# Softmax over rows of 512: three loads of 32 rows per partition, and the multiplications of six groups moved to GpSimd

## Chip, cores, metric

One core of a Trainium2 chip. The metric is the device time of one execution in microseconds (us).

## The reference

A softmax over the last axis, x of 16 x 1024 x 512 in fp32, result in fp32:

```python
x_max = np.max(x, axis=-1, keepdims=True)
exp_x = np.exp(x - x_max)
return (exp_x / np.sum(exp_x, axis=-1, keepdims=True)).astype(np.float32)
```

16,384 rows of 2 KB: 33.55 MB are read and 33.55 MB written. Each of the 128 partitions holds 128 rows.

## The kernel before

SBUF holds 96 rows per partition in one tile, so the last 32 rows are loaded over the first ones once these are stored. `CHUNKS` lists the loads as (rows, place). Work goes in groups of up to 8 rows: maxima on VectorE, exponentials with sums on ScalarE, reciprocal and multiplication on VectorE, then a store. The loads go out on the queue of SyncE, the stores on ScalarE's.

```python
CHUNKS = [
    (3, 0), (5, 3), (8, 8), (16, 16), (16, 32), (16, 48), (16, 64), (16, 80), (16, 0), (16, 16),
]
EARLY = 8                       # loads issued at the start
AFTER_STORE = {2: [8], 3: [9]}  # load 8 follows the store of chunk 2, load 9 that of chunk 3
STORE_ROWS = {3: 8, 4: 8, 5: 8} # stores of 8 rows in these chunks, else the whole chunk
# ... cut ...
    def scale(g):
        k, a, b, since = groups[g]
        recip = stats.tile([P, b - a], F32, name="recip", tag="recip")
        nc.vector.reciprocal(out=recip, in_=sums[g])
        for r in range(a, b):
            nc.vector.tensor_scalar_mul(
                out=place[k][:, r, :],
                in0=place[k][:, r, :],
                scalar1=recip[:, r - a : r - a + 1],
            )
        if since is not None:
            nc.scalar.dma_start(out=dst[k][:, since:b, :], in_=place[k][:, since:b, :])
        # ... cut: the loads of AFTER_STORE ...
        for g, (k, a, _, _) in enumerate(groups):
            # ... cut: groups 1 to 3 finish the group before first ...
            rowmax(g)
            exps(g)
            if waiting is not None:
                scale(waiting)
            waiting = g
```

The rows of one partition lie together in HBM, so a load of 16 rows is one run of 32 KB per partition, and the trace shows it as one packet of that size per partition, spread over 16 DMA engines.

## Time and profile before

| | before |
|---|---|
| median time | 161.45 us (six runs, 161.40 to 161.84) |
| span of the profiled execution | 159.6 us |
| bytes moved | 67.13 MB, 421 GB/s over the span |
| VectorE busy | 123.9 us, 78% |
| ScalarE busy | 93.3 us, 58% |
| GpSimd busy | 0.2 us |

The two slice rows, the chain and the groups are shown in the prediction below. In the lines of the profile DVE is VectorE, ACT ScalarE, POOL GpSimd and DMA a transfer; SPq is the queue of SyncE, which issues the loads.

### The profile page before, as it was taken

Reading aid. Unit: us, or ns where it says so; the run is one execution under the profiler, and the core shown is the slowest. Engines: PE = TensorE matmul, PEld = TensorE weight load, DVE = VectorE, ACT = ScalarE, POOL = GpSimd, SP = SyncE. Lnnn points to the kernel's source line nnn. Section 1 sums busy time; section 2 is a strip of 40 time slices with the busy share of each in tenths; the row PEclk is TensorE's granted clock in tenths of the full one; section 3 lists DMA queues with packets and bytes.
Section 4 is the critical chain, followed back from the end, with each engine's and each line's share of the span. In section 5 each row is a group of like instructions: output and inputs, shape, how many; then the busy total and the mean of one; then the engine's idle time right before and its main releaser. Section 6 shows DMA issues by size and latency. Waiting matters only on the chain.

```text
span 159.6 us, 511 instructions
## 1 busy us (share of the span) xinstructions
DVE 123.9 (78%) x162; ACT 93.3 (58%) x257; POOL 0.2 (0%) x4
## 2 busy tenths in 40 slices
DVE  0482880799699999999999999999999999853000
ACT  0717119207994959595958687776868595940000
POOL 0000000000000000000000000000000000000000
DMA  7999999899999999999899999999999999999993
GB/s 267 443 456 432 399 414 466 375 404 467 411 446 411 485 419 396 439 411 493 378 448 439 411 497 411 405 444 402 435 444 485 411 402 468 435 402 419 485 411 164
DMA packets 3315, 67.13 MB, mean 421 GB/s; under 512 B 368, under 2 KB 368, under 8 KB 624
## 3 DMA queue, kind: packets, MB, share of 16 engines
q1 hardware_dynamic: 1440, 33.56, 49.4%
q10 hardware_dynamic: 1872, 33.56, 49.0%
q14 instruction: 3, 0.02, 0.0%
HBM read 33.55 MB, written 33.55 MB: 421 GB/s over the span
## 4 chain that ended last, share of the span: by engine, by line
DVE 71%; ACT 14%; issue 3%; DMA 3%; DVEq 0%; ACTq 0%
DVE shift L125 39%; DVE held L147 30%; ACT held L133 14%; DMA held<-in_x_dram 3%; DVE recip L145 2%; DVEq L199 0%; ACTq L133 0%
## 5 line engine op out<-in xcount | busy, mean ns | idle before, releaser
L133 ACT ACTIVATE held<-held,shift 128x512 f32<-128x512 f32 x128 | 90.5, 708 | 43.4 <-DVE shift L125 33.3
L125 DVE TENSOR_REDUCE shift<-held 128x8 f32<-128x4096 f32 (+2 forms) x17 | 70.7, 4164 | 4.6 <-DMA held<-in_x_dram 4.6
L147 DVE TENSOR_SCALAR held<-held,recip 128x512 f32<-128x512 f32 x128 | 52.2, 482 | 0.6
L133 ACT ACTIVATION_READ_ACCUMULATOR held<-held,shift 128x1 f32 x128 | 23.9, 187 | 0.0
L145 DVE RECIPROCAL recip<-sums 128x8 f32<-128x8 f32 (+2 forms) x17 | 3.3, 195 | 15.8 <-ACT held L133 15.8
L133 ACT ACT_TABLE_LOAD x1 | 1.3, 1283 | 4.7 <-DMA held<-in_x_dram 4.7
L188 POOL MEMSET const-bfloat16-1.0<- 128x1 bf16 x1 | 0.1, 103 | 0.0
L188 POOL MEMSET const-uint8-127<- 128x1 uint8 x1 | 0.1, 102 | 0.0
L188 POOL MEMSET const-float32-1.0<- 128x1 f32 x1 | 0.1, 100 | 0.0
L188 POOL MEMSET const-float32-0.0<- 128x1 f32 x1 | 0.1, 99 | 0.2 <-issue 0.2
## 6 DMA issues: line engine op xcount, KB each, us to landing
held<-in_x_dram SPq DMA_DIRECT2D x7, 4096.0 KB, 41.8
out_dram<-held ACTq DMA_DIRECT2D x4, 4096.0 KB, 20.9
out_dram<-held ACTq DMA_DIRECT2D x7, 2048.0 KB, 35.3
held<-in_x_dram SPq DMA_DIRECT2D x1, 2048.0 KB, 11.7
held<-in_x_dram SPq DMA_DIRECT2D x1, 1280.0 KB, 7.2
out_dram<-held ACTq DMA_DIRECT2D x1, 1280.0 KB, 19.9
held<-in_x_dram SPq DMA_DIRECT2D x1, 768.0 KB, 4.6
out_dram<-held ACTq DMA_DIRECT2D x1, 768.0 KB, 15.6
```

The source lines that it names most:

```text
L125: nc.vector.reduce_max(out=shift[g], in_=place[k][:, a:b, :], axis=AX, negate=True)
L133: nc.scalar.activation(out=place[k][:, r, :], in_=place[k][:, r, :], func=EXP, bias=shift[g][:, r - a : r - a + 1], scale=1.0, accum_out=s ...
L145: nc.vector.reciprocal(out=recip, in_=sums[g])
L147: nc.vector.tensor_scalar_mul(out=place[k][:, r, :], in0=place[k][:, r, :], scalar1=recip[:, r - a : r - a + 1],)
L188: nc = _bacc.Bacc("TRN2", target_bir_lowering=False, num_devices=1)
```

## The change

The intent: fewer and larger loads, and VectorE is relieved of 48 of its 128 multiplications of one row. Six instructions of GpSimd take them, each 8 rows with the reciprocal broadcast along the row.

```diff
-CHUNKS = [
-    (3, 0), (5, 3), (8, 8), (16, 16), (16, 32), (16, 48), (16, 64), (16, 80), (16, 0), (16, 16),
-]
+CHUNKS = [(3, 0), (5, 3), (8, 8), (16, 16), (32, 32), (32, 64), (32, 0)]
-EARLY = 8
-AFTER_STORE = {2: [8], 3: [9]}
+EARLY = 6
+AFTER_STORE = {3: [6]}
-STORE_ROWS = {3: 8, 4: 8, 5: 8}
+STORE_ROWS = {3: 8, 4: 8, 5: 16, 6: 16}
+ON_POOL = (3, 5, 7, 9, 11, 13)
@@ scale @@
-        for r in range(a, b):
+        if g in ON_POOL:
+            nc.gpsimd.tensor_tensor(
+                out=place[k][:, a:b, :],
+                in0=place[k][:, a:b, :],
+                in1=recip.unsqueeze(2).to_broadcast([P, b - a, d]),
+                op=mybir.AluOpType.mult,
+            )
+        for r in () if g in ON_POOL else range(a, b):
             nc.vector.tensor_scalar_mul(
```

The groups and the sizes of the stores come out the same as before, 13 stores in the same order; only the loads differ.

## The prediction

> **What bounds the kernel now.** I read the page's slices first, then the DMA queues in stretches of 10 us, then the chain, then the costliest groups. The last two slice rows of the page:
>
> ```profile
> DMA  7999999899999999999899999999999999999993
> GB/s 267 443 456 432 399 414 466 375 404 467 411 446 411 485 419 396 439 411 493 378 448 439 411 497 411 405 444 402 435 444 485 411 402 468 435 402 419 485 411 164
> ```
>
> Only the first and the last slice are not full. The table of stretches has 433, 439, 425 and 436 GB/s for 40 to 60, 60 to 80, 80 to 100 and 100 to 120 us. The kernel must move 67.13 MB; at 0.433 MB/us that is 155 us of a span of 159.6. So the transfers are the floor, and some 4.6 us lie at the two ends.
>
> The chain of work that ended last tells another story:
>
> ```profile
> DVE 71%; ACT 14%; issue 3%; DMA 3%; DVEq 0%; ACTq 0%
> ```
>
> It ends with VectorE's last multiplication at 144.9 us, where the last store (4.19 MB) is issued. The landing records of the trace have that store landing at 158.9 and the one before it at 149.2. The gap of 9.7 us is 4.19 MB at 432 GB/s: the store queue was never empty. If the issue had come later than about 147 (149.2 less some 2 us of start-up), the end would have moved. So VectorE's chain is a second bound, with only some 2 us of slack behind the transfers. That is the number to keep in mind. One period of that chain, as the ordered chain prints it:
>
> ```profile
> 61.60 4.33 DVE shift L125
> 65.93 0.12 DVE recip L145
> 66.05 0.02 issue
> 66.07 3.26 DVE held L147 x8
> 69.33 4.33 DVE shift L125
> ```
>
> 7.73 us for a group of 8 rows, 15.46 for two; VectorE is full from 46 to 135 us. The groups give the parts:
>
> ```profile
> L133 ACT ACTIVATE held<-held,shift 128x512 f32<-128x512 f32 x128 | 90.5, 708 | 43.4 <-DVE shift L125 33.3 <-issue 10.2
> L125 DVE TENSOR_REDUCE shift<-held 128x8 f32<-128x4096 f32 x15 | 66.1, 4414 | 0.0
> L147 DVE TENSOR_SCALAR held<-held,recip 128x512 f32<-128x512 f32 x128 | 52.2, 482 | 0.6
> ```
>
> ScalarE needs 5.65 us for 8 rows (its exponentials start 0.705 us apart) and waits 33 us in all for VectorE's maxima.
>
> **What the Trainium skill says.**
> - "GPSIMD Engine Reference", section 3.1 Elementwise: a two-input multiplication runs at about 2.6 cycles an element, and 2048 fp32 elements took 4497 ns, because both inputs share one read port. No GpSimd arithmetic is in the trace of before, so nothing here confirms it.
> - "VectorE: DVE Perf Modes", section The perf-mode tier table: `tensor_scalar` on fp32 in SBUF gets the 2x mode, `tensor_reduce` stays at 1x. The trace agrees: 8 multiplications of 512 take 3.26 us, 0.41 us each, against 4414/8 = 0.55 us for each 512 reduced.
> - "SBUF — State Buffer", section Who interferes with whom: GpSimd and a VectorE instruction in that 2-port mode exclude each other; whoever starts first has the pair of ports for its whole instruction and the other "fully blocks". `tensor_reduce` on trn2 never contends. Not visible before.
> - "DMA: Bandwidth & Descriptors", section Queues, rings and completion order: each DMA engine takes turns between the queues a packet at a time. The trace agrees. From 50 to 60 us the load queue (q1, packets of 32 KB, 16 rows of 2 KB) and the store queue (q10, packets of 16 KB) moved:
>
> ```profile
> q1 hardware_dynamic: 110, 3.08, 71.4%
> q10 hardware_dynamic: 99, 1.36, 31.8%
> ```
>
> About two to one. The loads of 16 rows landed every 14.5 us (51.5, 66.1, 80.6, 95.1, 109.9), 0.289 MB/us, two thirds of 0.433.
>
> **The change part by part.**
> 1. Loads. Seven instead of ten, the same 33.55 MB. Packets of 64 KB (if one run per partition stays one packet) take 64/(64+10) of the engines against the store of 5 rows and 64/80 against one of 8. The rate can't rise: it is already flat at 433. What moves is who goes first. The load of 16 rows lands at 24.4 as before; the first of 32 rows needs 8.39 MB / (0.433 x 0.86) = 22.5 us more, so about 47. Before, its first half was there at 37.2. The second ends at 47 + 8.39 / (0.433 x 0.8) = 71. The stores wait meanwhile; those of rows 0 to 31 land at about 71 + 4.19/0.433 = 81, and the last load, 32 rows, starts then and lands at about 82 + 24 = 106. Before, the last load left at 82.5. Chunks of stores are the same sizes as before, and the last is still 16 rows.
> 2. VectorE loses 6 x 3.26 = 19.6 us: 48 of 128 multiplications.
> 3. GpSimd gets six multiplications of 128x4096. Estimate from the skill: 4497 x 2 = 9.0 us each (P), 54 us together. The engine is otherwise idle, so its busy time alone binds nothing. What matters is what waits on it.
> 4. Order. The instruction order after has, on VectorE: reciprocal of the odd group, maxima of the group after next, reciprocal of the even group, its 8 multiplications, the next maxima. On ScalarE, the store of an odd group of chunks 3 and 4 stands before the next exponentials, so ScalarE's queue waits for GpSimd there.
>
> **If the lock holds** (my main case): until the reciprocal of group 3, at 42.85, nothing moves. GpSimd runs 42.9 to 51.9. VectorE's maxima of group 5 wait for the load until 47 and end at 51.4, hidden under GpSimd. The multiplications of group 4 start at 51.9, when the ports are free, and end at 55.2. Maxima of group 6 to 59.5, reciprocal of group 5 at 59.8, GpSimd again at 59.9. The loop is P + 3.26 + 4.33 + 0.3 = 16.9 us for 16 rows, 1.4 more than 15.46. GpSimd starts at 42.9, 59.9, 76.8, 93.7, 110.6, 127.5. The last load (106) is needed at about 111: no wait. After the last start: 9.0, multiplications 3.3, maxima 4.4, exponentials of group 16 5.8, reciprocal 0.2, multiplications 3.3: 26.0. So the last store leaves at 153.5 instead of 144.9. Its queue is empty then, so it needs 2.3 (start-up, an estimate: the first load, 0.79 MB, landed at 4.6, of which 1.8 is data) plus 9.7, and the span ends 0.7 after the landing as before: 153.5 + 12.0 + 0.7 = 166.2. The timed figure lies 1.9 above the span (161.47 to 159.6): 168.1 us, 4% slower. Each microsecond of P moves it by 6 until the transfers bind again, at P about 8.0.
>
> **The rivals.**
> - No lock, or one so fine that VectorE slips in. Then the loop with single stores is bound by ScalarE (exponentials of the even group 5.7, wait for GpSimd 9.3 from its start, the next exponentials 5.7): about 15.0 for 16 rows; in the last two chunks, where a store goes with the even group, VectorE's two maxima, one set of multiplications and two reciprocals make about 12.5 to 13.5. With a wait for the last load (106) the last store leaves at about 142. The transfers bind as before: 159.6 and 161.4 us. For it: the loads and stores are at a flat 433 GB/s. Against: the skill's plain statement. It can't be much faster, since 155 us of data plus 2 to 3 at each end stay.
> - Larger loads starve the stores or the compute: the wait for the first 32 rows (47) and the late last load (106). I find both hidden. If 64 KB were split into packets of 32 KB the shares stay two to one, that load lands at 51.5 instead of 47, and group 5 is 4 us later: up to 4 us on the lock case, little in the other.
> - GpSimd slower than 9 us through the broadcast operand or blocked in its turn: every microsecond costs 6 in the end, 10 us each would give 174.
> - GpSimd faster than 8: the lock then costs nothing visible, about 161.5.
>
> **Range and chances.** The lock at P = 9 gives 168, no lock 161.4. The change is drawn so that VectorE is relieved, which would make no sense to its author with an engine that blocks it; that, and P unmeasured, keeps me from taking the first case whole. I lean to the lock a little over half and put the time between, at 165.0. The range: 160.2 (no lock, an easier tail) to 171.0 (lock with P of 9.5). Faster by 2% means 158.2, a span of 156.4 or 429 GB/s from the first microsecond to the last: 0.02. Slower by 2% means over 164.7, the lock with P above about 8.4: 0.57. The rest, 0.41, is within.
>
> **What would show each step.** A GpSimd multiplication of about 9.0 us in the groups. VectorE's multiplications of even groups waiting some 3 us after their reciprocal until GpSimd ends, or longer durations of single ones there, and a loop of 16.9; without the lock they follow at once. DMA slices below 9 after 125 us, and a last store issued at about 153 (lock) or 142 (none). Maxima of group 5 starting at 47 (64 KB packets) or 51 (32 KB). I am wrong if GpSimd's time is far from 9, if the last load lands late enough to stop VectorE, or if the rate of the DMA engines itself moves.

## More of the kernel before

One more view is needed later, the stretches of the trace of before: per line from:to, its length, busy time (and instructions) of VectorE, ScalarE and GpSimd, the TensorE clock, the mean busy share of the DMA engines, GB/s.

```profile
4.00:84.00 80.00, 65.79 (x82) 49.78 (x136) 0.00 (x0) 1.00 1.01 429
84.00:114.00 30.00, 29.86 (x39) 22.08 (x63) 0.00 (x0) 1.00 1.01 432
114.00:148.00 34.00, 28.29 (x44) 21.41 (x60) 0.00 (x0) 1.00 1.02 438
```

The rate is nearly the same while loads and stores share the engines (429 and 432 GB/s, the first two) and while stores run alone (438, the third).

## The result, and the profile after

| | before | after |
|---|---|---|
| median time | 161.45 us | 164.11 us (six runs, 163.93 to 164.42) |
| ratio, 95% interval | | 1.0163 (1.0149 to 1.0178) |
| span of the profiled execution | 159.6 us | 162.1 us |
| rate over the span | 421 GB/s | 414 GB/s |
| VectorE busy | 123.9 us | 108.5 us |
| GpSimd busy | 0.2 us | 42.3 us |
| last store issued, landed on its slowest engine | 144.9, 158.6 | 149.1, 160.9 |

After is 1.6% slower, inside the 2% that count as the same, though clear of noise.

The page of after, the chain and three groups (busy us, mean ns | idle before, what ended it):

```profile
DMA 63%; DVE 18%; ACT 9%; issue 1%; SPq 0%; DVEq 0%
...
L125 DVE TENSOR_REDUCE shift<-held 128x8 f32<-128x4096 f32 (+2 forms) x17 | 70.5, 4150 | 18.8 <-DMA held<-in_x_dram 18.8
L147 POOL TENSOR_TENSOR held<-held,recip 128x4096 f32<-128x4096 f32 x6 | 42.1, 7017 | 89.9 <-DVE recip L145 89.9
L154 DVE TENSOR_SCALAR held<-held,recip 128x512 f32<-128x512 f32 x80 | 36.5, 526 | 0.4
```

Four things to see. The chain, VectorE's in before (71%), now runs through transfers (63%). VectorE's maxima wait 18.8 us for loads; in before the same line had 4.6, all of it the first load. One GpSimd multiplication takes 7.02 us, not 9.0. And VectorE's mean multiplication went from 482 to 526 ns.

The last of these is the pair of ports that VectorE and GpSimd share (the prediction explains it; one_port and pool_rows below test it). VectorE and GpSimd in the timeline of after (start, us, what, count):

```profile
59.96 0.19 DVE L145 RECIPROCAL recip<-sums 128x8 f32<-128x8 f32 x1
60.07 4.37 DVE L125 TENSOR_REDUCE shift<-held 128x8 f32<-128x4096 f32 x1
65.86 0.20 DVE L145 RECIPROCAL recip<-sums 128x8 f32<-128x8 f32 x1 [1.42 <-ACT held L133]
66.10 4.21 DVE L154 TENSOR_SCALAR held<-held,recip 128x512 f32<-128x512 f32 x8
70.22 4.41 DVE L125 TENSOR_REDUCE shift<-held 128x8 f32<-128x4096 f32 x1
74.55 0.19 DVE L145 RECIPROCAL recip<-sums 128x8 f32<-128x8 f32 x1
```

```profile
60.23 7.02 POOL L147 TENSOR_TENSOR held<-held,recip 128x4096 f32<-128x4096 f32 x1 [10.56 <-DVE recip L145]
74.82 7.02 POOL L147 TENSOR_TENSOR held<-held,recip 128x4096 f32<-128x4096 f32 x1 [7.57 <-DVE recip L145]
```

The eight multiplications take 4.21 us where they took 3.26. Single records say where: the first lasts 1.43 us (66.10 to 67.53), the other seven 0.47 each, and GpSimd ends at 67.25. But with GpSimd at 7.0 us the wait is 1 us, and the loop for 16 rows is 14.59 us (59.96 to 74.55) against 15.46 before. VectorE gains from GpSimd; the lock is there and costs little.

Then VectorE stands still for the last load, which lands at 113.0:

```profile
103.72 0.18 DVE L145 RECIPROCAL recip<-sums 128x8 f32<-128x8 f32 x1
113.04 4.42 DVE L125 TENSOR_REDUCE shift<-held 128x8 f32<-128x4096 f32 x1 [9.13 <-DMA held<-in_x_dram]
```

That wait is the most conspicuous thing in the trace, and it puts the last store at 149.1 instead of 144.9. I took it for the cause at first. The completion records of the stores say otherwise. Each transfer leaves 16 of them, which I read as one per DMA engine; here is the last of the 16 for the last seven stores:

| store | 7th | 8th | 9th | 10th | 11th | 12th | 13th |
|---|---|---|---|---|---|---|---|
| before | 110.10 | 114.96 | 119.83 | 129.51 | 139.19 | 148.87 | 158.55 |
| after | 112.44 | 117.30 | 122.17 | 131.85 | 141.53 | 151.21 | 160.89 |
| difference | 2.34 | 2.34 | 2.34 | 2.34 | 2.34 | 2.34 | 2.34 |

The whole 2.3 us is there by 112 us, and nothing is added after it. The last store of after leaves at 149.1, while the slowest engine works on the 12th store until 151.2: that engine never waits for VectorE. So the loss is in the transfers and lies before 112 us. The stretches of after, the same ones as of before:

```profile
4.00:84.00 80.00, 58.00 (x57) 48.95 (x134) 21.05 (x3) 1.00 1.01 427
84.00:114.00 30.00, 19.41 (x18) 21.20 (x60) 14.03 (x2) 1.00 1.00 416
114.00:148.00 34.00, 30.03 (x39) 22.89 (x64) 7.02 (x1) 1.00 1.02 439
```

From 84 to 114 us the DMA engines count as just as busy (1.00 against 1.01) and move 416 GB/s instead of 432, which is 0.48 MB less in 30 us, or 1.1 us at 433 GB/s. Some 0.2 MB had been lost before 84 (2 GB/s over 80 us). These are means over 16 engines; the slowest lost 2.3 us, and about half of that was there by 82 us, as the completion records under one_big show. What happens at 84 to 114 is the last load:

```profile
82.45 0.02 SPq L120
...
82.64 30.38 DMA held<-in_x_dram
113.01 0.02 issue
```

SyncE waited until 82.5 us for the stores of the rows that the load overwrites. The load queue had been empty since 71.8, when the second load of 32 rows landed. The load is issued at 82.6 and its first packet starts at 87.2, 4.5 us later; once it runs, the packet records, spread over their durations, give 0.34 to 0.41 MB/us for some 10 us instead of 0.43. In before the load queue never ran dry until its end: load 9 (counted from 0) was issued at 82.46 while load 8 was in flight until 94.8.

**Theory**, as it stood before the experiments. A load queue that runs dry and starts again beside full store queues costs rate, on the slowest engine most; loads of 32 rows bring this about, and they lose a little rate themselves. The queue runs dry because one load of 32 rows must wait until all its rows are free. The last of the stores that free them landed at 82.10 in after and at 82.07 in before; but in before the half for rows 0 to 15 could leave at 53.4 and kept the queue full. (Packets of 64 KB also push the stores back: the third one landed at 72.4 instead of 53.0.) GpSimd and VectorE's late chain cost nothing. **Rivals:** GpSimd costs the time (ports, ScalarE's waits for GpSimd before a store); or VectorE's 9.1 us wait and the late last store do.

### The profile page after: what moved, and what is told of

Its sections match the earlier page's. It is cut to its first block, busy times and chain, and to the rows that moved or that the text cites. A ratio compares the mean times of both kernels' runs of the same rounds, so it can differ in the third digit from the quotient of the medians.

```text
span 162.1 us, 467 instructions
## 1 busy us (share of the span) xinstructions
DVE 108.5 (67%) x114; ACT 93.0 (57%) x257; POOL 42.3 (26%) x10
## 4 chain that ended last, share of the span: by engine, by line
DMA 63%; DVE 18%; ACT 9%; issue 1%; SPq 0%; DVEq 0%
DMA held<-in_x_dram 47%; DMA out_dram<-held 16%; DVE shift L125 11%; ACT held L133 9%; DVE held L154 6%; SPq L120 0%; DVE recip L145 0%; DVEq L206 0%
## 5 line engine op out<-in xcount | busy, mean ns | idle before, releaser
L125 DVE TENSOR_REDUCE shift<-held 128x8 f32<-128x4096 f32 (+2 forms) x17 | 70.5, 4150 | 18.8 <-DMA held<-in_x_dram 18.8
L147 POOL TENSOR_TENSOR held<-held,recip 128x4096 f32<-128x4096 f32 x6 | 42.1, 7017 | 89.9 <-DVE recip L145 89.9
L154 DVE TENSOR_SCALAR held<-held,recip 128x512 f32<-128x512 f32 x80 | 36.5, 526 | 0.4
```

The lines of the kernel that those rows point to most:

```text
L125: nc.vector.reduce_max(out=shift[g], in_=place[k][:, a:b, :], axis=AX, negate=True)
L147: nc.gpsimd.tensor_tensor(out=place[k][:, a:b, :], in0=place[k][:, a:b, :], in1=recip.unsqueeze(2).to_broadcast([P, b - a, d]), op=mybir.A ...
L154: nc.vector.tensor_scalar_mul(out=place[k][:, r, :], in0=place[k][:, r, :], scalar1=recip[:, r - a : r - a + 1],)
```

## The experiments

Ten kernels ran, all correct. Each ratio is against before in the same rounds.

| run | what | median us | ratio (95%) |
|---|---|---|---|
| after | | 164.11 | 1.0163 (1.0149 to 1.0178) |
| pool_only | loads of before, GpSimd of after | 161.47 | 0.9997 (0.9986 to 1.0009) |
| loads_only | loads of after, no GpSimd | 164.32 | 1.0175 (1.0162 to 1.0188) |
| split_last | after, last load as two of 16 | 165.45 | 1.0243 (1.0225 to 1.0260) |
| split_middle | after, middle loads as four of 16 | 163.34 | 1.0112 (1.0088 to 1.0136) |
| swap_last | before, last two loads change places | 162.29 | 1.0055 (1.0042 to 1.0069) |
| tail8_after | after, last store as two of 8 rows | 164.27 | 1.0178 (1.0156 to 1.0199) |
| one_big | one load of 32 rows, queue never dry | 162.68 | 1.0065 (1.0050 to 1.0080) |
| no_big | its control, without that load | 161.99 | 1.0037 (1.0018 to 1.0055) |
| one_port | VectorE's multiplication also writes its sum, meant to keep it from the 2-port mode | 169.05 | one run |
| pool_rows | GpSimd in single rows | 164.68 | one run |

one_big and no_big ran on another chip than the rest, each beside before on the same chip.

### Which half of the change: pool_only and loads_only

```diff
 # pool_only, against after: CHUNKS, EARLY, AFTER_STORE and STORE_ROWS of before; ON_POOL stays
 # loads_only, against after
-ON_POOL = (3, 5, 7, 9, 11, 13)
+ON_POOL = ()
```

> The ten loads of before, with the six GpSimd multiplications of after. Theory (the large loads cost the time): the transfers bind as in before, 161.4 us within 0.5; GpSimd 7.0 us each; the last store leaves at about 135 to 142 instead of 144.9 and lands no earlier; no wait of VectorE for a load after the first. Rival (the shared ports and ScalarE's wait for GpSimd cost the time): about 164, as after.

> The seven loads of after, all multiplications on VectorE. Theory (the large loads cost the time): the last load lands at about 113 again, VectorE waits for it some 3 us (it gets there at 47.9 + 8 x 7.73 = 109.7), and from there the 37.0 us of before to the last store: 150.0 instead of 149.1 in after, so about 165.0 us, 0.9 above after. Rival (GpSimd costs the time): about 161.5.

The loads carry the whole loss. pool_only is before to 0.1%, although the ports are contended as in after; its last store leaves at 139.4, 5.5 us before that of before, and lands at 158.59 against 158.55. The relief is real and the transfers hide it. loads_only came within 0.2 us of after. I had expected 0.9 us more, from a last store at 150.0; it left at 150.35 and cost only 0.2. That was the first sign that the time of the last store was not what counted.

### A miss: split_last, with split_middle

```diff
 # split_last, against after
-CHUNKS = [(3, 0), (5, 3), (8, 8), (16, 16), (32, 32), (32, 64), (32, 0)]
+CHUNKS = [(3, 0), (5, 3), (8, 8), (16, 16), (32, 32), (32, 64), (16, 0), (16, 16)]
-AFTER_STORE = {3: [6]}
+AFTER_STORE = {2: [6], 3: [7]}
 # split_middle, against after
-CHUNKS = [(3, 0), (5, 3), (8, 8), (16, 16), (32, 32), (32, 64), (32, 0)]
-EARLY = 6
-AFTER_STORE = {3: [6]}
-STORE_ROWS = {3: 8, 4: 8, 5: 16, 6: 16}
+CHUNKS = [(3, 0), (5, 3), (8, 8), (16, 16), (16, 32), (16, 48), (16, 64), (16, 80), (32, 0)]
+EARLY = 8
+AFTER_STORE = {3: [8]}
+STORE_ROWS = {3: 8, 4: 8, 5: 8, 8: 16}
```

> As after, but the last load of 32 rows is two of 16, the first of which waits for the stores of chunks 0 to 2 alone. Theory: no wait of VectorE for it, the last store leaves at about 142, only the rate lost to the two middle loads of 32 rows stays (some 0.2 MB behind before, 0.5 us): 161.9 to 162.6 us. Rival (the middle loads or GpSimd matter): 163.5 to 164.1.

> As after, but the two middle loads of 32 rows are four of 16; the last one stays 32 rows. Theory (the last load alone costs): the stores of rows 0 to 31 land at 82 as in before, the last load starts some 4 us after its issue and lands at about 112 to 113, the last store leaves at about 149: 163.3 to 164.1 us. Rival (middle loads matter): 161.5 to 162.5.

split_last did what it was made for: no late wait for a load, and the last store at 142.8, 6 us earlier than in after. Its waits for loads (us in total, times, longest) were:

```profile
DVE shift L125 <- DMA held<-in_x_dram: 10.2, 2, 5.8
```

The longest is for the first load of 32 rows. And it was the slowest of the kernels timed in rounds: 165.45 us, above both ranges (161.9 to 162.6 and 163.5 to 164.1). That refutes the idea that the late load harms through VectorE. Its loads ran dry twice: one was issued at 73.0 and started at 77.5, the next at 93.1 and started at 96.7. The slowest engine ended at 161.93, 3.4 us after that of before; the first engine to finish the last store did so at 158.48. In before these two lie 1.2 us apart. So the 16 engines no longer ran level.

split_middle (163.34 us, at the lower edge of the 163.3 to 164.1 expected), with one dry spell (issued at 81.5, started at 85.9) and one load of 32 rows, came out between: slowest engine at 159.98, 1.43 us behind, although VectorE waited 11.5 us for the last load, longer than in after.

```profile
DVE shift L125 <- DMA held<-in_x_dram: 15.9, 2, 11.5
```

(The waits of split_middle, in the same form.) A longer wait, a shorter time.

### A dry load queue alone: swap_last

```diff
 # against before
-(16, 80), (16, 0), (16, 16),
+(16, 80), (16, 16), (16, 0),
-AFTER_STORE = {2: [8], 3: [9]}
+AFTER_STORE = {3: [8, 9]}
```

> The kernel before, without GpSimd and without a load over 16 rows; only the places of its last two loads change sides, so that the ninth load has to wait for the stores of rows 16 to 31 (they land at about 82) while the eighth load has landed at about 80: the load queue runs dry and starts again. Theory (a load queue that starts again while stores fill the DMA engines loses rate, and the slowest engine most): first packet of the ninth load about 4.5 us after its issue at 82.5, some 0.2 to 0.5 MB behind before from then on, last store still issued at 144.9 with no new wait of VectorE, and the last engine ends 1 to 2.5 us later: 162.4 to 164 us. Rival (only packets of 64 KB or late work cost): 161.4 to 161.7.

The same transfers and the same instructions as before, in the same sizes; only the ninth load now needs rows that come free at 81. It was issued at 81.3, the load queue had been dry since 80.2, and its first packet started at 85.7. VectorE has no new wait and the last store leaves at 144.7. The time rose by 0.85 us, the slowest engine ended 0.79 us later (159.34), and the stretches of swap_last show the same mark as after, only weaker:

```profile
4.00:84.00 80.00, 65.99 (x82) 50.00 (x136) 0.00 (x0) 1.00 1.01 429
84.00:114.00 30.00, 29.86 (x39) 22.09 (x63) 0.00 (x0) 1.00 1.02 425
114.00:148.00 34.00, 28.05 (x43) 21.18 (x60) 0.00 (x0) 1.00 1.01 434
```

429 as before until 84, then 425 instead of 432. So a restart of the loads by itself costs this kernel some 0.85 us, with no load over 16 rows and no new wait of VectorE. It costs the engines alike, though, not the slowest most: the first of the 16 to finish the last store ended 0.91 us later in the profiled executions (158.23 against 157.32), the last one 0.79. My range began at 162.4; it was 162.29, just below it.

### The late last store: tail8_after

```diff
 # against after
-            ends = b == R or b - since >= STORE_ROWS.get(k, R)
+            ends = b == R or b - since >= (8 if k == 6 and a >= 16 else STORE_ROWS.get(k, R))
```

> As after, but the last 16 rows are stored as two of 8, so that a store is there 3.5 us earlier and the store queue has no gap at 149 us. Theory (the slowest DMA engine is never idle, it only got behind around the restart of the loads): no gain, 163.9 to 164.3 us. Rival (VectorE's late last store, and with it the 9 us wait for the last load, costs 0.7 us): 163.2 to 163.5.

No gain: 164.27 us; the interval of its ratio, 1.0156 to 1.0199, takes in the 1.0163 of after. The slowest engine ended at 160.83 against 160.89. The store queue had something to do from 143.7 us on and it did not matter, as the table of completions said.

### Packets of 64 KB without a dry queue: one_big and no_big

```diff
 # both against before
-SBUF_ROWS = 96
+SBUF_ROWS = 100
 # one_big
+CHUNKS = [(3, 0), (5, 3), (8, 8), (16, 16), (16, 32), (16, 48), (32, 64), (4, 96), (16, 0), (12, 16)]
+STORE_ROWS = {3: 8, 4: 8, 5: 8, 6: 16}      # EARLY and AFTER_STORE as in before
 # no_big
+CHUNKS = [(3, 0), (5, 3), (8, 8), (16, 16), (16, 32), (16, 48), (16, 64), (16, 80), (4, 96), (16, 0), (12, 16)]
+EARLY = 9;  AFTER_STORE = {2: [9], 3: [10]}
```

> The kernel before with four more rows of SBUF and loads of 3, 5, 8, 16, 16, 16, 32, 4, 16 and 12 rows: one load of 32 rows (packets of 64 KB) whose successor is already queued, so that the load queue should not run dry before the last load is issued. Theory A (packets of 64 KB by themselves lose rate beside stores): 0.3 to 0.6 us above no_big. Theory B (only a load queue that runs dry loses): equal to no_big within 0.2 us, about 161.5.

> The control of one_big: its load of 32 rows is two of 16, all else the same. No load over 16 rows, no dry queue: 161.4 to 161.6 us, as before; both theories say the same.

In both the load queue was never dry (the last load went out at 86.3 and 81.6 with the one before in flight until 98.5 and 102.2). The means are 162.57 and 162.04: 0.5 us for one load of 32 rows, in the range of theory A. The runs overlap (162.07 to 162.93, and 161.54 to 162.60), so by the times it is likely rather than shown. no_big was itself 0.4% above before, which I had not expected and can't explain. In the profiled executions the rate of one_big fell behind while its large load ran: 428 GB/s from 4 to 74 us, no_big 431. (Those two executions lie further apart than the means: 162.93 and 161.67 us.)

The completion records of runs whose load queue is empty at 82 us settle it for the middle loads. By then each engine has done the same work in all of them: the loads of the first 96 rows per partition and the first five stores. When the first and the last engine had done it:

| run | loads of 32 rows so far | first engine | last engine |
|---|---|---|---|
| swap_last | none | 79.73 | 80.78 |
| split_middle | none | 79.80 | 80.91 |
| after | two | 80.07 | 82.10 |
| loads_only | two | 80.04 | 82.24 |
| tail8_after | two | 80.02 | 82.05 |

Two loads of 32 rows cost the slowest engine some 1.2 us and the fastest 0.3, before any restart. GpSimd multiplies in split_middle and after and not in swap_last and loads_only; with and without it the last engine agrees within 0.14 us.

### The ports: one_port and pool_rows

```diff
 # one_port, against after: VectorE's multiplication also writes out its sum
-            nc.vector.tensor_scalar_mul(out=..., in0=..., scalar1=recip[...])
+            nc.vector.tensor_scalar(out=..., in0=..., scalar1=recip[...], scalar2=0.0,
+                op0=mybir.AluOpType.mult, op1=mybir.AluOpType.add, accum_out=unused[...])
 # pool_rows, against after: one tensor_tensor for each of the 8 rows
+            for r in range(a, b):
+                nc.gpsimd.tensor_tensor(out=place[k][:, r, :], ...)
```

> As after, but VectorE's multiplications also write out their sum[...]; they take some 0.6 us or more instead of 0.41 and an accumulator read. Theory (the pair of ports shared with GpSimd is what the first multiplication waits for): the first multiplication of groups 6, 8, 10, 12 and 14, issued while GpSimd runs, is as short as the others. Rival (it waits for something else, such as GpSimd's semaphore): still about 1 us longer than the others. The time is not the question; 164 to 168 us.

> As after, but each GpSimd multiplication is eight of one row (some 0.9 to 1.0 us each). Theory (the lock holds for one instruction): VectorE's multiplications get in between two of GpSimd's and each can wait up to one of them, so that both engines' instructions of that stretch stretch out, instead of one wait for the whole group. Rival (no lock): neither changes. About 164 us.

one_port, GpSimd and VectorE in the timeline:

```profile
62.60 7.02 POOL L149 TENSOR_TENSOR held<-held,recip 128x4096 f32<-128x4096 f32 x1 [8.52 <-DVE recip L147]
```

```profile
68.23 0.20 DVE L147 RECIPROCAL recip<-sums 128x8 f32<-128x8 f32 x1 [1.42 <-ACT held L135]
68.47 0.74 DVE L156 TENSOR_SCALAR_CACHE_REDUCE held<-held,recip 128x512 f32<-128x512 f32 x1
69.14 0.08 DVE L156 DVE_READ_ACCUMULATOR held<-held,recip 128x1 f32 x1
69.14 0.74 DVE L156 TENSOR_SCALAR_CACHE_REDUCE held<-held,recip 128x512 f32<-128x512 f32 x1
```

The first multiplication starts at 68.47 and takes 0.74 us like the next, while GpSimd runs until 69.62. The wait of after is gone with this slower form (0.74 us instead of 0.48), which I take to be outside the fast mode. (It is another instruction, so this is as near as I could come to the mode alone. The single run took 169.05 us, more than the 164 to 168 expected.)

In pool_rows GpSimd's rows take 1.04 us each. VectorE's multiplications that begin at 66.60 last 1.37, 1.26 and then 0.47 us, GpSimd's last row 1.22: VectorE gets in between two rows and holds up the next. The lock is taken for one instruction.

## Why the prediction was right or wrong

The measured 164.11 us lies in the range and 0.9 us from the point. That nearness is luck: 165.0 lay between two cases, 168 with the lock and 161.4 without, and the time came from neither.

- **The transfers are the floor, VectorE's chain close behind.** Right, and stronger than stated: in pool_only that chain ended 5.5 us earlier and nothing came of it. The slack was mis-sized: the start-up of 2.3 us does not follow from its own figures (4.6 less 1.8 is 2.8), and the last store of after started 0.85 us after its issue (149.12 to 149.97). In before the slowest engine finished the store ahead at 148.87, so the slack was about 3 us (an estimate from these figures), not 2.
- **P, GpSimd's multiplication, 9.0 us.** Mis-sized: 7.02 us. This was the term that made the lock expensive.
- **The lock.** Right in kind: VectorE's first multiplication waited for GpSimd's end, in groups 6, 8, 10 and 14 (1.43 us each); groups 4 and 12 came to theirs after GpSimd's end, because VectorE had waited for a load before; and one_port and pool_rows bear it out. With P at 7.0 the loop is 14.6 us instead of 16.9. The prediction itself said that below 8 the lock costs nothing visible, about 161.5 us, and pool_only measured 161.47.
- **Larger loads: "The rate can't rise: it is already flat at 433. What moves is who goes first."** This step failed. The rate did not rise; it fell (416 GB/s instead of 432 from 84 to 114 us). 2.3 us on the slowest engine are missing from the sum, and they are the whole result: some 1.2 us by 82 us, with the two middle loads of 32 rows, and about 1.1 after that, with the restart. The text listed a moving rate among what would prove it wrong, and gave it no size.
- **Packets of 64 KB stay whole, shares, first load of 32 rows at about 47, second at 71, issue of the last at 82.** Right: 47.9, 71.8 and 82.6.
- **The last load lands at 106.** Mis-sized: 113.0. The load started 4.5 us after its issue, on an empty queue beside a full one; then it needed 25.5 instead of 24. The chance that it stops VectorE was called hidden; it stopped VectorE for 9.1 us, and, as split_last and tail8_after show, that cost nothing.
- **A last store landing 12.0 us after its issue.** 149.12 to 161.24 by the landing record, so 12.1, but by luck: the wait for the slowest engine, busy until 151.21, took the place of the start-up.

The chances, 0.57 for slower by over 2%, leaned on the lock at P = 9 and were on the wrong side of the line.

What is shown: the loads cause the loss (pool_only, loads_only); it lies in the DMA engines before 112 us (completion records); a dry load queue costs 0.85 us here by itself (swap_last); the two middle loads of 32 rows cost the slowest engine 1.2 us (completion records at 82 us); neither the late store of after nor VectorE's wait costs anything (tail8_after, split_last, split_middle). As a sum over single effects, 0.85 for the restart and about 0.5 (one_big less no_big) for each of three large loads make 2.4 us of the 2.7 measured; the 0.5 is uncertain by nearly half. What stays open: why packets take longer around a restart and beside 64 KB packets, and which engine falls behind. The records do not say which engine a packet ran on.

No version beat the kernel before. pool_only equals it. With 155 us of data at the flat rate in 159.6, there was little to win.

## What to carry to other kernels

In a kernel bound by transfers, order the reuse of buffers so that the load queue always has its next transfer issued before the last has landed; here a restart cost 0.85 us. A larger load can break this order, because it must wait for the last of the rows that it overwrites and takes its share from the stores that free them, and here two loads of 32 rows cost the slowest engine 1.2 us by themselves. Do not take the longest wait of a compute engine for the cause: compare when the last DMA engine finishes each store, before and after, and see from which store on the difference stands. Moving work to an idle engine is worth nothing while the relieved engine already has slack.

## What the Trainium skill lacked or had wrong

- "GPSIMD Engine Reference", section 3.1 Elementwise: about 2.6 cycles an element and 4497 ns for 2048 fp32 elements with two inputs. Here a multiplication with a broadcast second operand took 7017 ns for 4096 elements, 1.71 ns each against 2.2; in rows of 512 it took 1039 ns, about 2.0 each. No run here has a full second operand, so this adds a case to the page's figure and does not refute it.
- "DMA: Bandwidth & Descriptors", section Queues, rings and completion order: turns by packets between queues agree with the shares here (the second load of 32 rows landed at 71.8, 71 by such shares), but the page does not say that a transfer on an empty queue starts late beside a full one: 4.5 us from issue to first packet (after), 4.4 (swap_last and the first in split_last), 3.6 (its second), and 3.7 for the first store of before beside a full load queue (10.17 to 13.84), against 0.85 for the last store of after, issued when the load queue was empty and the first engine idle.
- Same page: no word that the summed rate drops after such a start, 425 and 416 GB/s against 432 over 30 us, nor that large loads beside stores drive the engines apart: the first and the last lie 2.0 us apart at 82 us in after, 1.1 in swap_last, and 3.4 at the end of split_last.
- "SBUF — State Buffer", section Who interferes with whom: the exclusive lock for one instruction agrees. What the section lacks is how the wait looks in a trace: not as idle time before the instruction, but as a longer instruction, here 1.43 us instead of 0.47 in after, and 1.37 and 1.26 us between GpSimd's rows in pool_rows.
